# A two-layer decoder trunk: reciprocals by transposed rows, and the first two weight units multiplied together

## The chip, the cores and the metric

The kernel runs on one core of one Trainium2 chip. The core has a matrix engine (TensorE, PE in the profile, with its weight loads as PEld), a vector engine (VectorE, DVE), an activation engine (ScalarE, ACT), GpSimd (POOL) and a queue engine (SyncE, SP) that only starts transfers here. Each engine works through its own instructions in order; semaphores make it wait for others. The metric is the device time of one execution in microseconds (us), as the median of several runs; less is better.

## The reference

512 positions of width 1024 pass two layers. The change lies in the first (even) layer, whose mixer is:

```python
h = x @ w_in                                  # one projection
q_a, c_kv, q_idx, k_idx, w_idx, q_b, k_b, v_b, f_in = split(h)
q_lat = einsum('bshd,hrd->bshr', q_a, w_uk) * HEAD_DIM**-0.5
cum_f = cumsum(log_sigmoid(f_in + b_f))       # forget gates of heads B
# per block of 128 queries:
score = einsum('bth,bths->bts', w_idx, relu(q_idx . k_idx))   # 8 index heads
sel   = top_k(score, 128)                     # causal
oa = softmax(q_lat . c_sel + t5_bias) @ c_sel # 8 heads A, selected keys only
ob = softmax(q_b . k_b + cum_f - cum_f_keys) @ v_b            # 8 heads B
out = concat([oa @ w_uv, ob]) @ w_o
x = layer_norm(ALPHA * x + out); x = layer_norm(ALPHA * x + conv_ffn(x))
```

The second layer has a gated mixer and another such FFN. All data are float32.

## The kernel before

Every float32 operand of a product is split in two rounded parts, high and low, and a product is three matmuls (`mm3`: high x high, high x low, low x high). The splitting is one cast on ACT for the high part and one subtraction for the low part, on DVE, or on POOL for the units listed in `POOL_CUT`.

All weights are one stream `ws` of units of 128 x 1024. `Stream` loads a unit on SP's queue into one of three `raw` buffers (L60), and cuts it (L76, L80, L78 on POOL) into one of three pairs `whi`/`wlo`, or into a `quad`. Unit 0 holds index keys, forget gates and index weights of the query, units 1 to 4 the index queries, unit 5 the latent keys `c_kv`, units 6 to 9 the values of heads B, then pairs of queries and keys, and from unit 23 on the output projection.

At the start `load_x` (L131) loads x, transposed, in eight chunks of 128 x 512 behind the first unit, and cuts each. `proj` then multiplies unit 0 with all eight chunks, and the index queries follow, unit by unit (L373). Four transposes of the gates (L383) stand behind the index queries and ahead of the latent keys; they give `nfq` and `wi`, which the gate bias and the scores use. The scores (`scores`, L426) follow, then the choice of the 128 best keys in rounds on DVE (`choose`), which is threaded through the later work.

Attention runs over 16 heads (0 to 7 are heads B, 8 to 15 heads A) in the loop at L657. For each head the string `SEQ` gives the order in which the pieces are written: `L` logits of head h, `B` bias of head h+1 (POOL), `T` the ten transposes of the weights of head h-1 into the three-bank tile `tri` and their cut into `pt`, `S` the softmax of head h (`soft`: minimum on DVE, exponentials with their sums `den` on ACT; `soft2`: the reciprocals), `V` the values of head h-2, and digits for pieces of projections that fill PE in between. The values come out with features on partitions, while a reciprocal belongs to a position, so `rd` (128 x 4) must be turned into rows:

```python
nc.sync.dma_start(rd_d[h].rearrange("a b -> b a"), rd)                # soft2, L593
nc.sync.dma_start(rb[r], rd_d[h].rearrange("a b -> (a b)").partition_broadcast(64))   # values, L626
eng.tensor_tensor(out=t, in0=t, in1=rb, op=ALU.mult)                  # values, odd h, L634
nc.scalar.copy(o[0], t)                                               # L635
```

The write goes to DRAM with its last two dimensions exchanged; the read spreads a head's 512 numbers over 64 partitions. For an odd head the pair of heads is multiplied on POOL (the last on DVE) and cut into an `oq` quad, which the output projection (`out_ln`) takes. L631 copies a head's values out of PSUM.

The tile framework sets the semaphores and orders the instructions of each engine by a timeline of its own, so the order on an engine isn't quite that of the code.

Of the kernel before, what the change touches and what calls it, by code (L numbers as in the profile page):

```python
# [94 lines left out]
def _body(ctx, tc, A):  # L95
# [31 lines left out]

    xq = [[quad(), quad()], [quad(), quad()]]
    ws.load_to(1)

    def load_x(c):  # L131
        for j in range(2):
            r = temp()
            k = 2 * c + j
            nc.sync.dma_start(r, A["xT"][:, k])
            hi, lo = xq[0][k // 4][:, k % 4], xq[1][k // 4][:, k % 4]
            nc.scalar.copy(hi, r)  # L137
            nc.vector.tensor_tensor(out=lo, in0=r, in1=_f(hi), op=ALU.subtract)  # L138

    for c in range(4):  # L140
        load_x(c)
# [196 lines left out]
    with ExitStack() as m0:  # L338
# [7 lines left out]
        misc = quad()  # L346
        w = unit()
        p = proj(w, xq)
# [7 lines left out]
        e = temp()  # L356
        g = slice(64, 72)
# [5 lines left out]
        nc.vector.memset(e[g], 1.0)  # L363
        nc.vector.tensor_tensor_scan(out=cw[g], data0=e[g], data1=z[g], initial=0.0, op0=ALU.mult, op1=ALU.add)
        fk_d = dr.tile([NH, S], F32, name="fk_d")
        nc.gpsimd.dma_start(fk_d, cw[g])
        for k in range(5, 9):
            ws.big[base[0] + k] = quad
# [4 lines left out]
        for m in range(4):  # L373
            p = bank()
            half(unit(), xq, p, 128, S)
# [5 lines left out]
        p = bank()  # L381
        for n in range(NCH):
            nc.tensor.transpose(p[:, n * 128:n * 128 + 128], cw[:, n * 128:n * 128 + 128], ident)  # L383
        p3 = p.rearrange("p (a b) -> p a b", a=4)
        nfq = mc.tile([128, NCH, NH], F32)
        nc.scalar.mul(nfq, p3[:, :, 64:72], -1.0)
        wi = mc.tile([128, NCH, NH], F32)
        nc.scalar.mul(wi, p3[:, :, 96:104], float(NH ** -0.5))
# [26 lines left out]
                                compare_op=ALU.is_ge, fill=BIG, base=0, channel_multiplier=1)  # L415

# [158 lines left out]
        rd_d = dr.tile([16, NCH, 128], F32, name="rd_d")  # L575

        def soft(h):

            d, lg = st_[h]
            mn = sm.tile([128, 4], F32, name="mn")  # L580
            den = sm.tile([128, 4], F32, name="den")
            rd = sm.tile([128, 4], F32, name="rd")
            for j in range(NCH):
                dj = dslice(d, j)
                dve[0] = nc.vector.tensor_tensor_reduce(out=dj, in0=lg[j], in1=dj, scale=1.0, scalar=3e38,
                                               op0=ALU.add, op1=ALU.min, accum_out=mn[:, j:j + 1])
                nc.scalar.activation(dj, dj, AF.Exp, bias=mn[:, j:j + 1], scale=-1.0, accum_out=den[:, j:j + 1])
            st_[h] = (d, den, rd)

        def soft2(h):  # L590
            d, den, rd = st_[h]
            nc.vector.reciprocal(rd, den)
            nc.sync.dma_start(rd_d[h].rearrange("a b -> b a"), rd)  # L593
# [3 lines left out]
        def turn(h):  # L597
            d = st_[h][0]
            p = tri.tile([128, 1536], F32, name="tri")
            for i in range(NCH):  # L600
                for j in range(i, NCH):
                    o = PO[i] + (j - i) * 128
                    nc.tensor.transpose(p[:, o:o + 128], d[:, OFF[j] + i * 128:OFF[j] + i * 128 + 128], ident)
# [7 lines left out]
        def values(h):  # L611
# [4 lines left out]
            o = (oq[-1][:, i % 2], oq[-1][:, 2 + i % 2])  # L616
# [6 lines left out]
            if h % 2 == 0:  # L623
                ot[i] = (temp(), temp())
            t, rb = ot[i]
            nc.sync.dma_start(rb[r], rd_d[h].rearrange("a b -> (a b)").partition_broadcast(64))  # L626
# [5 lines left out]
            if h % 2 == 1:  # L632
                eng = nc.gpsimd if h < 15 else nc.vector
                eng.tensor_tensor(out=t, in0=t, in1=rb, op=ALU.mult)  # L634
                nc.scalar.copy(o[0], t)  # L635
                eng.tensor_tensor(out=o[1], in0=t, in1=_f(o[0]), op=ALU.subtract)
# [20 lines left out]
        for h in range(18):  # L657
            for c in SEQ:
# [4 lines left out]
                elif c == "B":  # L663
                    bias(h + 1)
                elif c == "S" and h < 16:
# [4 lines left out]
                elif c == "T" and 1 <= h <= 16:  # L670
                    turn(h - 1)
                elif c == "V" and h >= 2:
                    values(h - 2)
                elif c.isdigit():
                    fill(int(c))
# [190 lines left out]
```

## Time and profile before

| | us |
|---|---|
| runs, median of three | 1243.87 (1243.27 to 1244.43) |
| profiled execution, its own time | 1240.66 |
| its span | 1238.9 |
| PE busy in the span | 1168.8 (94%) |
| DVE, ACT, POOL busy | 685.8, 463.8, 201.9 |
| mean granted PE clock | 0.971 |

The profile's page is of one execution. A row of the timeline has the start and the duration of an instruction or of several alike, the engine, the source line, the operation with the tiles it writes and reads, their shapes, and in brackets how long the engine stood before it and what ended that. A row of the waits has the engine and line that waited, what it waited for, the total, the number of times and the longest. `SPq` rows are transfers started by SP's queue; the time to landing is in the list of issues.

### The profile page before, as it was taken

To read this page: it belongs to the slowest core of one execution; us is meant where nothing else is said; L and a number is where in the kernel's file an instruction comes from. 1 tells how busy PE (TensorE), PEld (TensorE's weight loads), DVE (VectorE), ACT (ScalarE), POOL (GpSimd) and SP (SyncE) were. 2 spreads that over 40 slices of the span, in tenths; PEclk is the share of its full clock that TensorE was granted. 3 is DMA by queue.
4 is the path that set the end of the run, shared out by engine and by line. 5 is a ranking of instruction groups with operands and counts; after the bars stand their busy time and mean duration, and the time that the engine had idled before them with its cause. 6 is when DMAs were issued, how large, how long until landed. Compare 5 with 4: busy or idle time off the path is not lost. (4 is left out here: it accounts for less than half of the span.)

```text
span 1238.9 us, 14423 instructions
## 1 busy us (share of the span) xinstructions
PE 1168.8 (94%) x5512; PEld 972.1 (78%) x5512; DVE 685.8 (55%) x1120; ACT 463.8 (37%) x693; POOL 201.9 (16%) x254
## 2 busy tenths in 40 slices
PE   7999998535999999999999999999999999999997
PEld 7787886434898888888888788888988888888886
DVE  6779854312656656656223885447565665662236
ACT  7525654422234443443222414233344344342121
POOL 3555653310300000000000420013000000000003
PEclk9999998767999999999999999999999999999999
DMA  6612511225213233234334313354123322344321
GB/s 227 216 66 69 94 14 30 60 61 179 93 60 98 90 102 102 88 106 147 121 118 170 111 52 121 126 184 166 60 94 102 102 88 99 102 140 149 102 85 69
DMA packets 49413, 132.03 MB, mean 107 GB/s; under 512 B 13800, under 2 KB 13808, under 8 KB 49344
## 3 DMA queue, kind: packets, MB, share of 16 engines
q1 hardware_dynamic: 44288, 115.39, 29.5%
q0 software_dynamic: 5056, 15.71, 4.1%
q8 instruction: 43, 0.70, 0.3%
q14 instruction: 26, 0.21, 0.1%
HBM read 122.63 MB, written 10.02 MB: 107 GB/s over the span
## 5 line engine op out<-in xcount | busy, mean ns | idle before, releaser
L156 PE MATMUL bank<-quad,whi 128*128 128x512 f32 (+2 forms) x932 | 356.5, 383 | 6.3 <-ACT quad L137 6.3
L157 PE MATMUL bank<-quad,whi 128*128 128x512 f32 (+2 forms) x932 | 355.6, 382 | 0.5 <-DVE quad L138 0.5
L158 PE MATMUL bank<-quad,wlo 128*128 128x512 f32 (+2 forms) x932 | 355.1, 381 | 0.0
L80 DVE TENSOR_TENSOR wlo<-raw,whi 128x1024 fp32r<-128x1024 f32 x150 | 183.6, 1224 | 291.3 <-ACT whi L76 290.6
L76 ACT CAST whi<-raw 128x1024 fp32r<-128x1024 f32 x161 | 169.6, 1053 | 262.0 <-PE bank L158 115.3
L156 PEld LDWEIGHTS bank<-quad,whi 128*128 128x128 f32 x932 | 176.1, 189 | 41.0 <-ACT quad L137 6.3
L157 PEld LDWEIGHTS bank<-quad,whi 128*128 128x128 f32 x932 | 176.5, 189 | 33.6 <-DVE quad L138 1.1
L158 PEld LDWEIGHTS bank<-quad,wlo 128*128 128x128 f32 x932 | 176.4, 189 | 32.9
L156 PE MATMUL bank<-whi,quad 128*128 128x512 f32 x388 | 151.5, 392 | 17.8 <-ACT temp L631 17.8
L157 PE MATMUL bank<-wlo,quad 128*128 128x512 f32 x388 | 151.6, 391 | 0.0
L158 PE MATMUL bank<-whi,quad 128*128 128x512 f32 x388 | 151.3, 390 | 0.0
L213 POOL DMA_DIRECT2D temp<-x x24 | 13.1, 548 | 567.9 <-ACT quadx L324 424.6
L156 PE MATMUL bank<-quad 128*128 128x512 f32 (+5 forms) x280 | 100.4, 362 | 2.3 <-DVE quad L195 1.4
L157 PE MATMUL bank<-quad 128*128 128x512 f32 (+5 forms) x280 | 98.7, 354 | 0.8 <-DVE quad L80 0.8
L156 PEld LDWEIGHTS bank<-whi,quad 128*128 128x128 f32 x388 | 73.2, 189 | 33.2 <-ACT temp L631 18.0
L158 PE MATMUL bank<-quad 128*128 128x512 f32 (+5 forms) x280 | 98.5, 353 | 0.0
L158 PEld LDWEIGHTS bank<-whi,quad 128*128 128x128 f32 x388 | 73.3, 189 | 15.3
L157 PEld LDWEIGHTS bank<-wlo,quad 128*128 128x128 f32 x388 | 73.3, 189 | 15.2
L293 DVE SCALAR_TENSOR_TENSOR temp<-bank,fcw,temp 128x511 f32<-128x511 f32 x88 | 65.4, 743 | 9.1 <-ACT temp L292 9.1
L80 DVE TENSOR_TENSOR quad<-raw,quad 128x1024 fp32r<-128x1024 f32 x24 | 31.2, 1306 | 68.3 <-ACT quad L76 67.9
L295 DVE SCALAR_TENSOR_TENSOR temp<-bank,fcw,temp 128x510 f32<-128x510 f32 x88 | 65.9, 748 | 3.0
L156 PEld LDWEIGHTS bank<-quad 128*128 128x128 f32 (+1 forms) x280 | 52.6, 189 | 14.6 <-issue 3.6
(148 smaller groups left out, 1293.0 us busy)
## 6 DMA issues: line engine op xcount, KB each, us to landing
raw<-in_ws_dram SPq DMA_DIRECT2D x192, 512.0 KB, 3.5
x<-temp SPq DMA_DIRECT2D x24, 256.0 KB, 2.0
temp<-x POOLq DMA_DIRECT2D x24, 256.0 KB, 3.2
temp<-in_xT_dram SPq DMA_DIRECT2D x8, 256.0 KB, 5.5
temp<-fk_d SPq DMA_DIRECT2D x8, 256.0 KB, 4.4
temp<-rd_d SPq DMA_DIRECT2D x16, 128.0 KB, 4.4
temp<-in_x_dram POOLq DMA_DIRECT2D x8, 256.0 KB, 8.3
quad<-in_ln_g_dram POOLq DMA_DIRECT2D x4, 512.0 KB, 6.0
```

Of the source, the lines that this page charges most:

```text
L76: nc.scalar.copy(hi, t)
L80: dve[0] = nc.vector.tensor_tensor(out=lo, in0=t, in1=_f(hi), op=ALU.subtract)
L156: nc.tensor.matmul(out, a[0], b[0], start=first, stop=False)
L157: nc.tensor.matmul(out, a[0], b[1], start=False, stop=False)
L158: return nc.tensor.matmul(out, a[1], b[0], start=False, stop=last)
L213: nc.gpsimd.dma_start(t, src[n * 128:n * 128 + 128, hf * 512:hf * 512 + 512])
L293: nc.vector.scalar_tensor_tensor(out=t[:, 1:], in0=p[:, :S - 1], scalar=cw[:, j, 1:2], in1=t[:, 1:], op0=ALU.mult, op1=ALU.add)
L295: nc.vector.scalar_tensor_tensor(out=t[:, 2:], in0=p[:, :S - 2], scalar=cw[:, j, 0:1], in1=t[:, 2:], op0=ALU.mult, op1=ALU.add)
```

## The change

There are four edits. The reciprocals of two heads are gathered in one tile of 128 x 8, transposed by PE in `turn`, behind the ten transposes of an odd head, into a free part of `tri`, copied by ACT and written by ACT's queue as eight rows of 512 B. Both reads of the pair (still by SP) are issued when its second head's values are done, and the division is a step of its own, `D`, two heads later (`divide`); it is on POOL for pairs 0 to 3 and on DVE for the others. At the start, the first two units are loaded in halves between the x chunks, and the products of both go through the chunks together, after seven products of a zeroed tile whose result isn't used. The transposes of the gates move behind the latent keys. `POOL_CUT` begins at unit 10 instead of 5.

```diff
-SEQ = "L2BT2SV2"
-POOL_CUT = range(5, 23)
+SEQ = "L2BT2SDV2"
+POOL_CUT = range(10, 23)
+WARM = 7
...
+    FIRST = 2
+    misc = quad()
...
-    ws.load_to(1)
...
+    nc.vector.memset(_f(misc[:, 0]), 0.0)
+    w0 = [(rawp.tile([128, 1024], F32, name="raw"), wp.tile([128, 1024], FR, name="whi"),
+           wp.tile([128, 1024], FR, name="wlo")) for _ in range(FIRST)]
+
+    def load_w(u, hf):
+        c = slice(hf * 512, hf * 512 + 512)
+        raw, hi, lo = (t[:, c] for t in w0[u])
+        nc.sync.dma_start(raw, A["ws"][u][:, c])
+        nc.scalar.copy(hi, raw)
+        nc.vector.tensor_tensor(out=lo, in0=raw, in1=_f(hi), op=ALU.subtract)
...
+    load_w(0, 0)
+    load_x(0)
+    load_w(1, 0)
+    for k in (1, 2, 3):
+        load_x(k)
+    load_w(0, 1)
+    load_x(4)
+    load_w(1, 1)
+    for k in (5, 6, 7):
+        load_x(k)
...
-        w = unit()
-        p = proj(w, xq)
+        q = bank()
+        for _ in range(WARM):
+            nc.tensor.matmul(q, misc[:, 0, :128], misc[:, 0], start=True, stop=True)
+        p0 = [bank() for _ in range(FIRST)]
+        for k in range(8):
+            for u in range(FIRST):
+                a = 128 if u else 0
+                w = w0[u][1:]
+                mm3(p0[u][:, a:], wk(w, k * 128, k * 128 + 128), xk(xq, k, a), k == 0, k == 7)
+        p = p0[0]
...
-        rd_d = dr.tile([16, NCH, 128], F32, name="rd_d")
+        rd_d = dr.tile([8, 2 * NCH, 128], F32, name="rd_d")
...
         def soft2(h):
-            d, den, rd = st_[h]
-            nc.vector.reciprocal(rd, den)
-            nc.sync.dma_start(rd_d[h].rearrange("a b -> b a"), rd)
+            d, den = st_[h]
+            if h % 2 == 0:
+                rds[h // 2] = sm.tile([128, 8], F32, name="rd")
+            o = 4 * (h % 2)
+            nc.vector.reciprocal(rds[h // 2][:, o:o + 4], den)
...
+            if h % 2 == 1:
+                nc.tensor.transpose(p[:8, 1280:1408], rds.pop(h // 2), ident)
+                row = temp()[:8, :128]
+                nc.scalar.copy(row, p[:8, 1280:1408])
+                nc.scalar.dma_start(rd_d[h // 2], row)
...
-            nc.sync.dma_start(rb[r], rd_d[h].rearrange("a b -> (a b)").partition_broadcast(64))
...
             if h % 2 == 1:
-                eng = nc.gpsimd if h < 15 else nc.vector
-                eng.tensor_tensor(out=t, in0=t, in1=rb, op=ALU.mult)
-                nc.scalar.copy(o[0], t)
-                eng.tensor_tensor(out=o[1], in0=t, in1=_f(o[0]), op=ALU.subtract)
+                rb = temp()
+                for e in range(2):
+                    nc.sync.dma_start(rb[64 * e:64 * e + 64], rd_d[i, 4 * e:4 * e + 4].rearrange(
+                        "a b -> (a b)").partition_broadcast(64))
+                ot[i].append(rb)
+
+        def divide(i):
+            t, rb = ot.pop(i)
+            q = oq[i // 2]
+            o = (q[:, i % 2], q[:, 2 + i % 2])
+            eng = nc.gpsimd if i < 4 else nc.vector
+            eng.tensor_tensor(out=t, in0=t, in1=rb, op=ALU.mult)
+            nc.scalar.copy(o[0], t)
+            eng.tensor_tensor(out=o[1], in0=t, in1=_f(o[0]), op=ALU.subtract)
...
-        for h in range(18):
+        for h in range(20):
...
+                elif c == "D" and h >= 4 and h % 2 == 0:
+                    divide(h // 2 - 2)
```

The source lines of the changed kernel are other numbers. SP's queue in the attention, before: L593 writes a head's reciprocals, L626 reads them back, L60 loads a weight unit.

```order
L626 DMA temp<-rd_d 64x512
L60 DMA raw<-in_ws_dram 128x1024 x2
L593 DMA rd_d<-rd 128x4x1
L626 DMA temp<-rd_d 64x512
L60 DMA raw<-in_ws_dram 128x1024
L593 DMA rd_d<-rd 128x4x1
```

The same queue now, with L671 for a read and L61 for a weight unit:

```order
L61 DMA raw<-in_ws_dram 128x1024 x2
L671 DMA temp<-rd_d 64x512 x6
L61 DMA raw<-in_ws_dram 128x1024
L671 DMA temp<-rd_d 64x512 x2
L61 DMA raw<-in_ws_dram 128x1024 x3
L671 DMA temp<-rd_d 64x512 x4
```

The writes have left the queue, and reads stand together in pairs.

ACT at the end of the attention, before: L587 are exponentials, L194 cuts the transposed weights, L631 copies values out, L635 cuts a divided pair, L76 casts a weight unit.

```order
L587 ACTIVATE d,den<-d,mn 128x384
L587 ACTIVATE d,den<-d,mn 128x512
L194 CAST pt<-tri 128x1280
L631 COPY temp<-bank 64x512
L635 CAST quad<-temp 128x512
L76 CAST quad<-raw 128x1024 x2
L194 CAST pt<-tri 128x1280
```

ACT at the same place now; L640 copies a pair's row of reciprocals, L641 issues its write, L618 are exponentials, L213 cuts the weights, L667 copies values out, L681 cuts a divided pair, L77 casts a unit.

```order
L640 COPY temp<-tri 8x128
L213 CAST pt<-tri 128x1280
L618 ACTIVATE d,den<-d,mn 128x128
L618 ACTIVATE d,den<-d,mn 128x256
L641 DMA rd_d<-temp 8x128
L618 ACTIVATE d,den<-d,mn 128x384
L667 COPY temp<-bank 64x512
L618 ACTIVATE d,den<-d,mn 128x512
L213 CAST pt<-tri 128x1280
L667 COPY temp<-bank 64x512
L681 CAST quad<-temp 128x512
L77 CAST quad<-raw 128x1024 x2
```

The write of the pair of heads 12 and 13 stands between exponentials of head 15, and the cut L681 behind it is the cut of that same pair.

PE at the start, before, where unit 0 ends and unit 1 begins (L156, L157, L158 are the three products of `mm3`):

```order
L156 MATMUL bank<-quad,whi 128x512
L157 MATMUL bank<-quad,whi 128x512
L158 MATMUL bank<-quad,wlo 128x512
L156 MATMUL bank<-quad,whi 128x384
L157 MATMUL bank<-quad,whi 128x384
```

PE's first rows now (L368 are the products of the zeroed tile, L175, L176, L177 those of `mm3`):

```order
L368 MATMUL bank<-quad 128x512 x7
L175 MATMUL bank<-quad,whi 128x512
L175 MATMUL bank<-quad,whi 128x384
L176 MATMUL bank<-quad,whi 128x512
L177 MATMUL bank<-quad,wlo 128x512
L176 MATMUL bank<-quad,whi 128x384
```

The products of the two units alternate from the first chunk on.

More of the change, by code (lines that the diff above doesn't have):

```diff
@@ L125, in unit, with load_x @@
         return ws.get(i)
+    FIRST = 2
+    misc = quad()
     xq = [[quad(), quad()], [quad(), quad()]]
-    ws.load_to(1)
[L131 to L141, printed above, removed]
+    nc.vector.memset(_f(misc[:, 0]), 0.0)
[7 more added lines that the diff above has]
+        nc.vector.tensor_tensor(out=lo, in0=raw, in1=_f(hi), op=ALU.subtract)
+    def load_x(k):
+        r = temp()
+        nc.sync.dma_start(r, A["xT"][:, k])
+        hi, lo = xq[0][k // 4][:, k % 4], xq[1][k // 4][:, k % 4]
+        nc.scalar.copy(hi, r)
+        nc.vector.tensor_tensor(out=lo, in0=r, in1=_f(hi), op=ALU.subtract)
+    load_w(0, 0)
[8 more added lines that the diff above has]
+        load_x(k)
+    ws.loaded = ws.split_to = base[0] = FIRST
     ident = cst.tile([128, 128], F32)
@@ L356, in _body @@
         e = temp()
+        one = temp()
         g = slice(64, 72)
@@ L362, in _body @@
         nc.vector.scalar_tensor_tensor(out=z[g], in0=z[g], scalar=0.0, in1=e[g], op0=ALU.min, op1=ALU.subtract)
-        nc.vector.memset(e[g], 1.0)
-        nc.vector.tensor_tensor_scan(out=cw[g], data0=e[g], data1=z[g], initial=0.0, op0=ALU.mult, op1=ALU.add)
+        nc.gpsimd.memset(one[g], 1.0)
+        nc.vector.tensor_tensor_scan(out=cw[g], data0=one[g], data1=z[g], initial=0.0, op0=ALU.mult, op1=ALU.add)
         fk_d = dr.tile([NH, S], F32, name="fk_d")
         nc.gpsimd.dma_start(fk_d, cw[g])
-        for k in range(5, 9):
-            ws.big[base[0] + k] = quad
+        for k in range(6, 10):
+            ws.big[k] = quad
         qi = [quad(), quad()]
@@ L373, in _body @@
         for m in range(4):
-            p = bank()
-            half(unit(), xq, p, 128, S)
+            if m < FIRST - 1:
+                p = p0[1 + m]
+            else:
+                p = bank()
+                half(unit(), xq, p, 128, S)
             for s, (a, b) in enumerate(((slice(0, 64), slice(64, 128)), (slice(64, 128), slice(0, 64)))):
@@ L379, in _body @@
                                                in1=_f(qi[s][a, m, lt]), op0=ALU.mult, op1=ALU.subtract)
[L381 to L388, printed above, removed]
         p = proj(unit(), xq)
@@ L415, in _body @@
                                 compare_op=ALU.is_ge, fill=BIG, base=0, channel_multiplier=1)
+        p = bank()
+        for n in range(NCH):
+            nc.tensor.transpose(p[:, n * 128:n * 128 + 128], cw[:, n * 128:n * 128 + 128], ident)
+        p3 = p.rearrange("p (a b) -> p a b", a=4)
+        nfq = mc.tile([128, NCH, NH], F32)
+        nc.scalar.mul(nfq, p3[:, :, 64:72], -1.0)
+        wi = mc.tile([128, NCH, NH], F32)
+        nc.scalar.mul(wi, p3[:, :, 96:104], float(NH ** -0.5))
         sel = [None] + [mc.tile([128, 128 * (j + 1)], F32, name=f"sel{j}") for j in (1, 2, 3)]
@@ L573, in logits @@
             st_[h] = (d, lg)
-        rd_d = dr.tile([16, NCH, 128], F32, name="rd_d")
+        rd_d = dr.tile([8, 2 * NCH, 128], F32, name="rd_d")
+        rds = {}
         def soft(h):
@@ L615, in values @@
             i = h // 2
-            o = (oq[-1][:, i % 2], oq[-1][:, 2 + i % 2])
             v = vB if h < 8 else vA
@@ L623, in values @@
             if h % 2 == 0:
-                ot[i] = (temp(), temp())
-            t, rb = ot[i]
-            nc.sync.dma_start(rb[r], rd_d[h].rearrange("a b -> (a b)").partition_broadcast(64))
+                ot[i] = [temp()]
+            t = ot[i][0]
             for k in range(NCH):
@@ L671, in _body @@
                     turn(h - 1)
-                elif c == "V" and h >= 2:
+                elif c == "V" and 2 <= h <= 17:
                     values(h - 2)
```

4 lines of the change are left out of this document (1 added, 3 removed).

## The prediction

> **What bounds the kernel now.** I read the waits of TensorE (PE) first, then its busy time by stretch, then the queue that the releases lead to. The span:
>
> ```profile
> span 1238.9 us, 14423 instructions
> ```
>
> The profiled execution took 1240.66 us, 1.8 us more than its span and 3.2 us less than the 1243.87 us median of the timed runs. The sum below is made against 1240.66 and then moved by these 3.2 us.
>
> Busy time by stretch (columns: stretch, its length, PE, PEld, DVE, ACT, POOL busy with counts, granted clock, DMA share, GB/s), and below it the longest waits:
>
> ```profile
> 100.00:199.80 99.80, 99.79 (x539) 80.03 (x537) 68.66 (x181) 53.87 (x124) 52.41 (x82) 0.99 0.27 46
> 199.80:292.85 93.05, 42.79 (x210) 34.63 (x210) 28.30 (x62) 33.54 (x70) 23.96 (x35) 0.69 0.27 63
> ...
> POOL temp L634 <- DMA temp<-rd_d: 45.9, 4, 20.0
> ACT quad L635 <- POOL temp L634: 45.2, 5, 13.0
> ...
> PE bank L156 <- ACT pt L194: 26.0, 3, 14.4
> ```
>
> PE never stands between 100 and 199.8 us, then is busy less than half of the next 93 us, at a granted clock of 0.69. The waits chain: PE waits for ACT's cast of the transposed weights (L194), ACT stands in L635 for POOL, POOL stands in L634 for the reciprocals' read from DRAM. ACT and POOL run in order, so what is queued behind L635 and L634 waits too.
>
> Where the read is late shows in SP's queue (start, duration) and the time from issue to landing:
>
> ```profile
> 188.98 0.54 SPq L593 DMA_DIRECT2D rd_d<-rd  x1
> 199.97 0.45 SPq L626 DMA_DIRECT2D temp<-rd_d  x1
> ...
> 284.81 0.45 SPq L626 DMA_DIRECT2D temp<-rd_d  x1
> 285.32 18.75 SPq L60 DMA_DIRECT2D raw<-in_ws_dram  x7
> ...
> x<-temp SPq DMA_DIRECT2D x24, 256.0 KB, 2.0
> temp<-rd_d SPq DMA_DIRECT2D x16, 128.0 KB, 4.4
> rd_d<-rd SPq DMA_DIRECT2D x16, 2.0 KB, 11.0
> fk_d<-temp POOLq DMA_DIRECT2D x1, 16.0 KB, 3.9
> ```
>
> A write of 2 KB of reciprocals (L593) takes 11.0 us, because its transposed pattern is 512 pieces of one number. The read of that head (L626) stands behind it in SP's queue and waits for its landing, and the next head's write stands behind the read. From 199.97 to 284.81 there are eight reads, heads 8 to 15, so a head costs 84.84/7 = 12.1 us in this stretch, whatever the engines could do. The weights of the next stage stand behind the last read, at 285.32:
>
> ```profile
> 291.15 1.04 ACT L76 CAST quad<-raw 128x1024 fp32r<-128x1024 f32 x1 [20.85 <-DMA raw<-in_ws_dram]
> ...
> 292.85 0.80 PE L156 MATMUL bank<-whi,quad 128*128 128x512 f32 x1 [17.80 <-ACT temp L631]
> ```
>
> **The change part by part: the reciprocals.** Removed are 16 writes of 11.0 us and their places in SP's queue. Added are eight PE transposes, eight small ACT copies, eight writes of 8 rows of 512 B issued by ACT, and 8 x 2 reads (16 as before); the division of a pair comes two heads later. How much PE needs in the stretch when nothing holds it, from the starts of values (V), logits (L) and turn (T) of one head and of what follows each:
>
> ```profile
> 184.28 0.40 PE L156 MATMUL bank<-pt,quad 128*128 128x512 f32 x1
> ...
> 186.12 0.45 PE L156 MATMUL bank<-quad,whi 128*128 128x512 f32 x1
> ...
> 229.40 0.33 PE L156 MATMUL bank<-quad 64*128 64x128 f32 x1
> ...
> 231.50 0.45 PE L156 MATMUL bank<-pt,quad 128*64 128x512 f32 x1
> ...
> 252.69 1.32 PE L603 MATMUL tri<-ident,d 128*128 128x128 f32 x10
> 253.76 0.47 PE L157 MATMUL bank<-pt,quad 128*64 128x512 f32 x1
> ```
>
> V 1.84, L 2.10, T 1.07 us. The 210 instructions of the stretch are seven V, six T, four L and six of the twelve products of a fifth (1.2 us), and 11 products of projections at 0.23: 12.9 + 6.4 + 9.6 + 2.5 = 31.4 us. So 93.05 - 31.4 = 61.6 us is waiting and half clock, and no more can be won here.
>
> What is late next is the last but one pair (heads 12 and 13). Its row is written by ACT behind two exponentials of head 15, so its chain starts about where L of head 15 is read. Before that point PE has 31.4 less two T and three V (7.7) = 23.7 us of work. ACT's 33.54 us in the row above hold what had piled up behind L635 and the casts of the tail, so it needs about as much; with 2 us for waits between the two the point lies at 199.8 + 25.7 = 225.5. From there: the write, between 2.0 (x<-temp, a wide write of SP) and 3.9 us (fk_d<-temp, eight rows, but POOL's queue), with the 11.0 of the scattered write as the far end; I take 2.0, since ACT's queue is of SP's kind and the piece is smaller. Two issues of 0.45 and 4.4 to landing make 7.3, with releases 7.8, the division 0.7: ACT's copy can start 8.5 us after that point. What follows it is in the trace already, for the same pair:
>
> ```profile
> 266.06 0.62 ACT L635 CAST quad<-temp 128x512 fp32r<-128x512 f32 x1 [12.96 <-POOL temp L634]
> 266.58 1.99 ACT L76 CAST quad<-raw 128x1024 fp32r<-128x1024 f32 x2
> 268.60 1.23 ACT L194 CAST pt<-tri 128x1280 fp32r<-128x1280 f32 x1
> ...
> 274.63 0.41 PE L158 MATMUL bank<-pt,quad 128*128 128x128 f32 x1
> ```
>
> From ACT's copy at 266.06 to the end of the last V at 275.04 are 9.0 us, with PE waiting and then at half clock; 0.8 for the copy that frees the last bank. So PE enters the output projection at 225.5 + 8.5 + 9.0 + 0.8 = 243.8 instead of 292.85: **-49.0 us**, at most -60.8 (PE never waits, less the new transposes). The weights are loaded by then, since SP no longer holds them. The eight transposes of the reciprocals take a tenth of a T each: **+0.8**. ACT's eight issues are not seen before; at the 0.54 of SP's first row above they are 4 us of a queue that has room outside the tail: 0 in the sum, 4 in the range. The divisions on POOL (pairs 0 to 3) and DVE come two heads, some 16 us, after the row is made, against a chain of 8: nothing.
>
> **The start.** The rows: first product, pitch cold, pitch warm, the second unit, its successor; and the loads.
>
> ```profile
> 6.27 0.80 PE L156 MATMUL bank<-quad,whi 128*128 128x512 f32 x1 [6.27 <-ACT quad L137]
> ...
> 8.64 0.63 PE L156 MATMUL bank<-quad,whi 128*128 128x512 f32 x1
> 9.06 0.63 PE L157 MATMUL bank<-quad,whi 128*128 128x512 f32 x1
> ...
> 13.43 0.40 PE L156 MATMUL bank<-quad,whi 128*128 128x512 f32 x1
> ...
> 15.51 0.33 PE L156 MATMUL bank<-quad,whi 128*128 128x384 f32 x1
> ...
> 19.70 0.33 PE L156 MATMUL bank<-quad,whi 128*128 128x384 f32 x1
> ...
> 5.00:10.00 5.00, 3.18 (x7) 2.20 (x8) 4.00 (x6) 3.93 (x7) 0.34 (x1) 1.00 1.03 352
> ```
>
> Products of 512 columns follow each other at 0.42 us until about 13 and then at 2.08/9 = 0.23 (nine from 13.43 to 15.51); the second unit's 24 take 4.19. Now both units' products share each x chunk. The first needs 0.26 MB less (half a weight unit), 0.75 us at 352 GB/s, and half a cast, 0.5: it starts at 5.0. All 3.15 MB must land: 2.36 MB more than the 0.79 of the old first product (there by 5.6) at 352 GB/s is 12.3; the last chunk's cast, remainder and six products put the end at 14.8. PE alone needs 24 x 0.23 + 4.19 = 9.7 us from 5.0: 14.7. I take 15.7 for some cold products and imperfect overlap: 19.7 - 15.7 = **-4.0 us** (-4.9 to +3.1, see the cold rival). The seven dummies (7 x 0.42 = 2.9 us) stand where PE only waits and cost nothing unless they outlast 5.0; SP's twelve issues run ahead of the landings as its nine did.
>
> On the clock: PE ran cold for some 6.6 us after its first product here. If the dummies begin at 1.5, that puts the warm clock at 8.1, 1.5 us of loss at most, inside my 1.0. [...]
>
> **The scores.** The gates' transposes (four, 0.4 us) and two small copies now stand directly ahead of the scores, up to 0.5 us of delay for DVE's first row there. POOL_CUT moves five remainders from POOL to DVE:
>
> ```profile
> 39.23 5.99 PE L426 MATMUL bank<-quad 128*128 128x256 f32 x34
> 46.71 5.12 PE L426 MATMUL bank<-quad 128*128 128x512 f32 x14 [1.48 <-ACT temp L428]
> ...
> 40.95 2.00 DVE L431 TENSOR_SCALAR sel<-temp,wi 128x256 f32<-128x256 f32 x1 [1.36 <-ACT temp L428]
> ...
> 38.07 4.72 POOL L78 TENSOR_TENSOR wlo<-raw,whi 128x1024 fp32r<-128x1024 f32 x2
> ...
> L80 DVE TENSOR_TENSOR wlo<-raw,whi 128x1024 fp32r<-128x1024 f32 x150 | 183.6, 1224 | 291.3 <-ACT whi L76 290.6
> ```
>
> The 48 score products need 16 x (0.23 + 0.17 + 0.115) = 8.3 us and take 39.23 to 51.83, 12.6. DVE's first small row takes 2.00 us while POOL cuts a unit and ends when POOL does. With five cuts fewer in POOL's backlog (2.36 us each) that overlap mostly goes; DVE's five (1.22 each) fall before 36 us, where it has room. Between 0 and -4.3, less the 0.5: I take **-2.0**, the middle, for DVE's own rows stay. PE is full from there to 199.8, so both gains pass on.
>
> Sum: -49.0 + 0.8 - 4.0 - 2.0 = -54.2; 1240.66 - 54.2 = 1186.5, and 3.2 more for the median: **1189** (1189.7). All after the attention is as before.
>
> **Rivals.** *Late reads* (0.13): the 11.0 us is the price of any write of rd_d, not of its pieces. Then each chain is 9 us longer: 9 on the last pair and, with two heads at some 11 us against a chain of 17, 6 each on pairs 4 and 5: 21 back, 1210. For it: ACT still waits in order at each pair's cut. Against: fk_d, also eight rows, lands in 3.9.
>
> *Cold start* (0.10): gaps between x chunks keep the clock low, so the two units take 24 x 0.42 + 24 x 0.32 (three quarters of the columns) = 17.8 us from 5.0 and end at 22.8: +3.1 instead of -4.0, 1197. For it: in the 93 us stretch a few microseconds of waiting brought half clock back. [...]
>
> *Slower* (0.04): PE now waits in its own order for a reciprocal at eight turns, with the next head's products behind it. It decides from 54.2/8 = 6.8 us per turn on, at 1250 from 7.6.
>
> ```profile
> 227.69 0.18 DVE L592 RECIPROCAL rd<-den 128x4 f32<-128x4 f32 x1 [0.88 <-ACT d L587]
> ...
> 232.76 1.32 PE L603 MATMUL tri<-ident,d 128*128 128x128 f32 x10
> ```
>
> For head 13 the reciprocal is there 6 us before the ten transposes end, so the wait should be nothing.
>
> *No change* (0.03): SP still stands in reads whose rows wait in ACT's queue, and a head costs 12 us again: 1244.
>
> **How the numbers follow.** My case has 0.70, with its own range 1176 to 1202: 60.8 in place of 49.0 and 4.9 in place of 4.0 at the low end, 8 us more for the last pair's chain (3.9 for 2.0, ACT's issues, a POOL-like landing) and no gain at the scores at the high end. The range must take in the cold start and half of the late reads: 1174 to 1209, which leaves out about 0.2. 0.2% (2.5 us) is about what a measurement of this kernel can tell from no change: faster 0.93, same 0.03, slower 0.04.
>
> **What would show it.** After: no PE wait on L194 over 4 us before the last pair; POOL's division without a long wait; rd_d's write landing in 2 to 4 us; SP's raw loads no longer behind reads; one PE gap of 5 to 8 us ahead of the output projection; PE's second unit done near 15.7. I am wrong if a row lands near 11 us, if DVE's or ACT's order makes a new wait per pair, or if the clock stays low until 20 us.

## The result, and the profile after

The changed kernel took 1185.84 us (median; 1182.65 to 1191.79) against 1243.57 us of the kernel before on the same chip: ratio 0.9549, 95% interval [0.9501, 0.9597]. On two more chips the ratio was 0.9613 [0.9590, 0.9636] and 0.9602 [0.9584, 0.9621]. The forecast, 1189.7 against 1243.87, is a ratio of 0.9564 and lies between these. The profiled execution took 1182.65 us, 58.0 us less than that of before; it is the shortest of the fourteen executions of the changed kernel on record, so what follows shows it at its best.

The span, and TensorE's busy time by stretch in the changed kernel (columns as before: length, PE, PEld, DVE, ACT, POOL, granted clock, DMA share, GB/s):

```profile
span 1180.9 us, 14445 instructions
...
100.00:199.80 99.80, 99.80 (x551) 80.20 (x550) 73.40 (x187) 60.38 (x136) 56.62 (x89) 1.00 0.20 63
199.80:236.20 36.40, 31.45 (x196) 25.32 (x194) 25.16 (x56) 26.89 (x59) 11.64 (x21) 1.00 0.30 93
```

What was 93.05 us with 42.79 of work at a clock of 0.69 is now 36.40 us with 31.45 of work at 1.00. The longest waits of PE (total, times, longest):

```profile
PE bank L457 <- ACT far L430: 1.8, 1, 1.8
PE bank L175 <- ACT pt L213: 1.6, 1, 1.6
...
PE bank L175 <- DVE quad L214: 1.4, 1, 1.4
PE bank L175 <- ACT whi L140: 1.3, 1, 1.3
PE bank L175 <- ACT temp L667: 1.2, 1, 1.2
PE tri L636 <- DVE pt L214: 1.2, 2, 1.0
```

No wait is longer than 1.9 us; 14.4 us for one cut (L194) and 17.8 ahead of the output projection are gone. The last but one pair of heads, from the timeline of ACT, SP, DVE and PE:

```profile
219.98 0.25 ACT L640 COPY temp<-tri 8x128 f32<-8x128 f32 x1 [0.96 <-PE tri L638]
...
220.27 0.27 ACTq L641 DMA_DIRECT2D rd_d<-temp  x1
221.26 0.39 ACT L618 ACTIVATE d<-d,mn 128x128 f32<-128x128 f32 x1
...
221.58 1.08 SPq L671 DMA_DIRECT2D temp<-rd_d  x2
...
226.95 0.68 DVE L680 TENSOR_TENSOR temp<-temp 128x512 f32<-128x512 f32 x1
...
236.20 0.50 PE L175 MATMUL bank<-whi,quad 128*128 128x512 f32 x1 [1.16 <-ACT temp L667]
```

and the DMA issues of the reads (KB each, median us to landing):

```profile
temp<-rd_d SPq DMA_DIRECT2D x16, 128.0 KB, 3.1
```

The row's write is issued at 220.27. The first read of it waits for that write and starts at 221.58, so this write landed in at most 1.3 us; over the eight pairs of heads the first read starts 1.3 to 3.6 us behind the write's issue. The division at 226.95 waits for no DMA, and PE enters the output projection at 236.20 instead of 292.85: -56.65 us, of which -2.06 were there when the scores ended.

The start and the scores of the changed kernel, from its timeline:

```profile
1.52 3.35 PE L368 MATMUL bank<-quad 128*128 128x512 f32 x7 [1.52 <-DVE mhalf L169]
5.12 0.79 PE L175 MATMUL bank<-quad,whi 128*128 128x512 f32 x1 [0.24 <-ACT quad L147]
7.20 0.69 PE L175 MATMUL bank<-quad,whi 128*128 128x384 f32 x1 [1.29 <-ACT whi L140]
...
19.55 0.34 PE L175 MATMUL bank<-quad,whi 128*128 128x384 f32 x1
...
42.10 7.66 PE L457 MATMUL bank<-quad 128*128 128x256 f32 x40 [1.82 <-ACT far L430]
42.56 1.12 DVE L462 TENSOR_SCALAR sel<-temp,wi 128x256 f32<-128x256 f32 x1 [0.15 <-ACT temp L459]
49.60 0.39 PE L175 MATMUL bank<-quad 128*128 128x512 f32 x1
```

The stretch from 45 to 50 us (columns as above), first of the kernel before:

```profile
45.00:50.00 5.00, 3.52 (x9) 2.46 (x9) 4.69 (x9) 3.54 (x8) 2.34 (x3) 0.72 0.63 217
```

and of the changed kernel:

```profile
45.00:50.00 5.00, 5.00 (x25) 4.31 (x24) 4.79 (x12) 4.70 (x11) 1.97 (x2) 1.00 0.32 117
```

The first real product starts at 5.12 as forecast, but the next waits 1.29 us for the second unit's first half. The pitch (the time from the start of one product of 512 columns to that of the next) stays at 0.42 until 12.9 as it did before, and the third unit starts at 19.55 instead of 19.70. The scores end 2.06 us earlier; in this execution the clock there was 1.00, in that of before 0.72.

### The profile page after: what moved, and what is told of

It reads as the page before. It is cut to its first block, busy times and chain, and to the rows that moved or that the text cites. A ratio compares the mean times of both kernels' runs of the same rounds, so it can differ in the third digit from the quotient of the medians.

```text
span 1180.9 us, 14445 instructions
## 1 busy us (share of the span) xinstructions
PE 1158.8 (98%) x5527; PEld 965.7 (82%) x5527; DVE 690.8 (59%) x1133; ACT 465.5 (39%) x703; POOL 186.5 (16%) x244
## 5 line engine op out<-in xcount | busy, mean ns | idle before, releaser
L175 PE MATMUL bank<-quad,whi 128*128 128x512 f32 (+2 forms) x932 | 355.2, 383 | 1.5 <-ACT whi L140 1.3
L177 PE MATMUL bank<-quad,wlo 128*128 128x512 f32 (+2 forms) x932 | 354.5, 380 | 0.0
L176 PE MATMUL bank<-quad,whi 128*128 128x512 f32 (+2 forms) x932 | 354.4, 380 | 0.0
L77 ACT CAST whi<-raw 128x1024 fp32r<-128x1024 f32 x159 | 167.5, 1053 | 258.2 <-PE bank L177 110.2
L175 PEld LDWEIGHTS bank<-quad,whi 128*128 128x128 f32 x932 | 175.7, 189 | 37.0 <-ACT whi L140 1.8
L177 PEld LDWEIGHTS bank<-quad,wlo 128*128 128x128 f32 x932 | 176.0, 189 | 32.5 <-issue 0.4
L176 PEld LDWEIGHTS bank<-quad,whi 128*128 128x128 f32 x932 | 176.2, 189 | 32.2
L175 PE MATMUL bank<-whi,quad 128*128 128x512 f32 x388 | 150.7, 390 | 1.2 <-ACT temp L667 1.2
L176 PE MATMUL bank<-wlo,quad 128*128 128x512 f32 x388 | 151.0, 389 | 0.0
L177 PE MATMUL bank<-whi,quad 128*128 128x512 f32 x388 | 150.8, 389 | 0.0
L232 POOL DMA_DIRECT2D temp<-x x24 | 13.1, 548 | 568.1 <-ACT quadx L343 424.6
L175 PE MATMUL bank<-quad 128*128 128x512 f32 (+5 forms) x280 | 99.9, 361 | 1.9 <-DVE quad L214 1.4
L176 PE MATMUL bank<-quad 128*128 128x512 f32 (+5 forms) x280 | 98.3, 352 | 0.6 <-DVE quad L81 0.6
L177 PE MATMUL bank<-quad 128*128 128x512 f32 (+5 forms) x280 | 97.7, 350 | 0.0
L175 PEld LDWEIGHTS bank<-whi,quad 128*128 128x128 f32 x388 | 72.8, 188 | 16.4 <-ACT temp L667 1.3
L177 PEld LDWEIGHTS bank<-whi,quad 128*128 128x128 f32 x388 | 72.8, 188 | 15.2
L176 PEld LDWEIGHTS bank<-wlo,quad 128*128 128x128 f32 x388 | 72.9, 188 | 14.8
L175 PEld LDWEIGHTS bank<-quad 128*128 128x128 f32 (+1 forms) x280 | 52.3, 188 | 14.6 <-issue 3.2
L311 ACT ACTIVATE temp<-bank,fcw 128x512 f32<-128x512 f32 x88 | 60.0, 681 | 10.8 <-PE bank L177 10.8
```

The source lines that it names most:

```text
L77: nc.scalar.copy(hi, t)
L175: nc.tensor.matmul(out, a[0], b[0], start=first, stop=False)
L176: nc.tensor.matmul(out, a[0], b[1], start=False, stop=False)
L177: return nc.tensor.matmul(out, a[1], b[0], start=False, stop=last)
L232: nc.gpsimd.dma_start(t, src[n * 128:n * 128 + 128, hf * 512:hf * 512 + 512])
L311: nc.scalar.mul(t, p, cw[:, j, 2:3])
```

## The experiments

Ratios are to the kernel before, run beside each set; the intervals are 95%. The sets ran on different chips, so they are compared by these ratios; the spread of a set is its longest execution less its shortest.

**Which part of the change.** First the reciprocals alone: the kernel before with the row, the later division (on VectorE from pair 4 on) and the sequence `L2BT2SDV2`, nothing else.

> The kernel before with only the reciprocals changed (one transposed row a pair, written by ScalarE's queue, division two heads later); start, gates' transposes and remainders as before. Theory 1: nearly the whole gain is here. TensorE reaches the output projection some 54.6 us earlier than the 292.85 of before, at about 238, and the time is about 1188, 2 us above the changed kernel. Rival (the prediction's sizes): 48.2 us, at 244.6, time about 1195, with the missing 6 us coming from the start and the scores by some way that the first products do not show.

Measured 1184.87 us, ratio 0.9564 [0.9539, 0.9588], so 54.0 us (51 to 57) of 1239.47. PE enters the output projection here:

```profile
239.40 0.50 PE L156 MATMUL bank<-whi,quad 128*128 128x512 f32 x1 [1.57 <-ACT temp L636]
```

That is 53.45 us earlier than before, 0.83 of them from ahead of the attention. Theory 1 holds: this part alone is as good as the whole change. Its four executions spread over 2.7 us, at a mean granted clock of 0.997 in each.

Then everything but the reciprocals: the new start, `POOL_CUT = range(10, 23)` and the gates' transposes at their new place.

> The kernel before with only the new start (two units together, seven dummies), the gates' transposes behind the latent keys and the remainders from unit 10 on; reciprocals as before. Theory 1: TensorE leaves the scores some 2 us earlier, and since it is full until 199.8 the heads bound by SyncE's queue start 2 us earlier too: about 1241.5, ratio 0.998. Rival 1: the chain of SyncE's queue swallows it, 1243.6. Rival 2 (the prediction's sizes): 6 us, 1237.6.

Measured 1235.93 us, ratio 0.9976 [0.9961, 0.9991]: 1.1 to 4.8 us. That is the size of theory 1, but not its way: the trace leaves the scores at 51.58, only 0.1 us before that of the kernel before, with a stretch of low clock between 40 and 55 in both. SP's reads of heads 8 to 15 start 2.15 us earlier for head 8 and 4.68 earlier for head 15 (197.82 and 280.13). The gain is small and real; what moves these reads stays open.

Then the changed kernel with the old start:

```
-    load_w(0, 0); load_x(0); load_w(1, 0); ...      (WARM dummies, two units together)
+    ws.load_to(1); load_x(c) for c in range(4)      (unit 0 whole, then unit 1)
```

> The changed kernel with the old start: the first unit whole, its product complete before the second unit is loaded, no dummies. Theory 1: the new start gives 0.2 us, because the clock stays low until about 13 us in both; second unit done near 19.7 and the time within 1 us of the changed kernel. Rival (the prediction's size): the new start is worth 4 us somewhere, 4 us above the changed kernel.

Measured 1188.32 us, 0.9597 [0.9573, 0.9621]: no more than the changed kernel on the other two chips. Its third unit starts at 19.39, so against the 19.55 of the changed kernel's first trace the new start with its seven dummies is worth nothing. But its trace shows another thing, at the end of the attention (ACT and PE):

```profile
241.78 1.04 ACT L77 CAST quad<-raw 128x1024 fp32r<-128x1024 f32 x1 [2.99 <-DMA raw<-in_ws_dram]
242.84 0.58 ACT L638 COPY temp<-bank 64x512 f32<-64x512 f32 x1
...
243.48 0.80 PE L157 MATMUL bank<-whi,quad 128*128 128x512 f32 x1 [5.50 <-ACT temp L638]
```

The copy that frees the last bank stands behind a cast that waits for weights; PE first reads such weights at 267.4, since four units of 24 products at 0.23 come first. PE waits 5.50 us and starts the projection at half pace (0.80). In the changed kernel one cast stands ahead of the copy, not two.

**Why the reciprocals gain.** Three ways to a part of it. The write on another queue:

```
-            nc.sync.dma_start(rd_d[h].rearrange("a b -> b a"), rd)
+            nc.scalar.dma_start(rd_d[h].rearrange("a b -> b a"), rd)
```

> The kernel before with one edit: the scattered write of each head's reciprocals is issued by ScalarE's queue instead of SyncE's. The write still has 512 pieces and still lands some 11 us after its issue; only SyncE's order is freed, so that the next head's write does not stand behind a read that waits. Theory 1 (order on SyncE's queue makes the 12.1 us a head): the reads come closer than 12 us, a head costs 6 to 9 us, and about half to two thirds of the gain comes back: 1208 to 1220. Rival (the 11 us of the landing set a head whatever the queue, since ScalarE and GpSimd run in order and wait for each read): a head still costs 12 us, 1243.

Measured 1203.94 us, 0.9718 [0.9692, 0.9745]. The write's issues, and from the timeline SP's last eight reads (the first, and the last four) and PE:

```profile
rd_d<-rd ACTq DMA_DIRECT2D x16, 2.0 KB, 12.6
```

```profile
185.74 0.44 SPq L626 DMA_DIRECT2D temp<-rd_d  x1
...
223.87 20.09 SPq L626 DMA_DIRECT2D temp<-rd_d  x4
...
255.62 0.79 PE L156 MATMUL bank<-whi,quad 128*128 128x512 f32 x1 [1.53 <-ACT temp L631]
```

The write still lands only after 12.6 us, yet the eight reads start from 185.74 to 243.5, 8.25 us a head instead of 12.1, and 37.2 of the 56.65 us are won. So a landing of 11 us made 12 us a head only through the order on SP's queue, and one word of code gives two thirds of the gain. A fast write left on SP's queue, the other way to break that chain, was not tried.

The division two heads later (on VectorE from pair 4 on), with the scattered writes left on SP:

> The kernel before with one part of the change alone: the division of a pair comes two heads later; the scattered writes stay a head each, on SyncE's queue. Theory 1: SyncE's order still makes a head cost 12 us from head 8 on, so the delay wins little: 1232 to 1244. Rival: it was ScalarE and GpSimd standing in order behind each read that held TensorE, and the delay alone brings half of the gain or more, 1215 or less.

Measured 1236.0 us in one execution, beside 1238.26 of before. SP's reads of heads 8 and 15:

```profile
199.09 0.45 SPq L625 DMA_DIRECT2D temp<-rd_d  x1
...
280.23 0.45 SPq L625 DMA_DIRECT2D temp<-rd_d  x1
```

(280.23 - 199.09)/7 = 11.6 us a head, and a time within the range of the kernel before (1235.38 to 1242.25): the delay alone wins little or nothing.

And the changed kernel with the row undone:

```
-                nc.tensor.transpose(p[:8, 1280:1408], rds.pop(h // 2), ident)
-                row = temp()[:8, :128]
-                nc.scalar.copy(row, p[:8, 1280:1408])
-                nc.scalar.dma_start(rd_d[h // 2], row)
+                nc.scalar.dma_start(rd_d[h // 2].rearrange("a b -> b a"), rds.pop(h // 2))
```

> The changed kernel with one part undone: no transposed row; a pair's reciprocals are written straight from the 128 x 8 tile, 1024 pieces of one number, at the same place of ScalarE's queue, and the division still comes two heads later. Theory 1: the write takes 11 to 20 us instead of 2; pairs 0 to 5 are hidden by the two heads' delay up to about 16 us, and the last pair's chain is 9 to 18 us longer: TensorE reaches the output projection at 250 to 262 and the time is 1198 to 1212. Rival: with its own queue and the delay the pieces no longer matter, 1186 to 1190.

Measured 1196.75 us, 0.9664 [0.9637, 0.9691]. The write's issues, and from the timeline the end of the attention on DVE, SP, ACT and PE:

```profile
rd_d<-rd ACTq DMA_DIRECT2D x8, 4.0 KB, 11.4
```

```profile
227.44 0.69 DVE L677 TENSOR_TENSOR temp<-temp 128x512 f32<-128x512 f32 x1 [7.17 <-DMA temp<-rd_d]
...
245.94 1.01 SPq L61 DMA_DIRECT2D raw<-in_ws_dram  x2
...
250.23 1.04 ACT L77 CAST quad<-raw 128x1024 fp32r<-128x1024 f32 x1 [9.00 <-DMA raw<-in_ws_dram]
251.93 0.80 PE L175 MATMUL bank<-whi,quad 128*128 128x512 f32 x1 [6.17 <-ACT temp L664]
```

That is just under the 1198 to 1212 of theory 1. 1024 pieces land in 11.4 us, as 512 did in 11.0, so between these the time did not follow the number of pieces. The division that waits 7.17 us is that of heads 10 and 11, the last but two pair: its read starts at 214.39 and lands only at 227.4, while the next pair's scattered write, issued at 216.48, is under way. The last pair's write is issued at 233.18 and lands 11.4 us later; its reads hold SP until then, the weights behind them come at 245.94, and the cast that waits for them holds the last copy. PE enters the projection 12 to 16 us later than in the three traces of the changed kernel. By the ratios the row is worth 0.005 to 0.0115 of 1238, 6 to 14 us, and its place is the end of the attention.

**Why the start gains nothing, and why executions differ.** The changed kernel again, with and without dummies, and with one edge that puts the casts of the projection's later weights behind the last copy:

```
+        if self.hold is not None and i >= self.hold[0]:
+            self.tc.add_manual_dep(c.ins, self.hold[1].ins.name, AFTER, ...)     (tail_order)
```

> The changed kernel once more, beside its variants, to see its spread between executions. Theory 1: its executions fall into two groups some 5 us apart. The copy that frees the last bank of the attention stands behind a cast that waits for weights from DRAM; when these land late, TensorE waits over 3 us ahead of the output projection and runs its first products there at half pace. Expected 1182 to 1184 or 1188 to 1192 on the chip of the first comparison, about 4 us less on the chip where the kernel before took 1239.5. Rival: one group, spread evenly.

> The changed kernel without any dummy. Theory 1: the seven dummies do nothing, because the gaps behind them start the count again: first product at 5.1, pitch 0.23 from about 12.7, second unit done at 19.5 to 20, as with seven. Rival: the seven dummies already save something, and without them the pitch stays at 0.42 until 14 or later and the second unit ends after 21.

> The changed kernel with thirteen dummy products instead of seven, so that TensorE works from 1.5 to about 7 us without a gap. Theory 1: what kept the pitch at 0.42 us until 12.7 were the gaps of 0.24 and 1.29 us behind the seven dummies; the pitch drops to 0.23 some 4.5 to 6 us after 1.5, so before 8.3, and the second unit ends where the last x chunk lets it, at 15.5 to 17 instead of 19.7. Rival 1: dummies on zeros don't count and the pitch drops at 12.3 to 13.3 as in all runs so far; second unit done at 20.5 or later, since the first product starts 2 us later. Of the 3 us won at the start, 1 to 3 reach the end, so that the time is 1 to 3 us less than the changed kernel's on the same chip.

> The changed kernel with one ordering edge: the casts of the output projection's later weights stand behind the copy that frees the last bank of the attention on ScalarE. Theory 1: that copy starts within 0.6 us of the last value product in every execution, TensorE waits at most 1.3 us ahead of the output projection, its first products there follow at 0.23 us, and the slower group of executions is gone: median 0 to 4 us below the changed kernel's, spread under 3 us. Rival: the spread has another cause and stays at 5 to 9 us.

Measured: 1190.33 us (1186.49 to 1191.39), 0.9613; without dummies 1186.54 in one execution; with thirteen 1186.84 (1182.95 to 1190.78), 0.9590 [0.9563, 0.9616]; with the edge 1184.79 (1181.74 to 1188.48), 0.9573 [0.9551, 0.9595]. The landmarks of the traces, in us:

| | pitch 0.23 from | scores begin | next product behind the scores | output projection begins | span |
|---|---|---|---|---|---|
| before | 12.9 | 39.23 | 51.66 | 292.85 | 1238.9 |
| changed | 12.9 | 39.07 | 49.60 | 236.20 | 1180.9 |
| changed, second time | by 7.4 | 36.77 | 51.12 | 239.97 | 1185.9 |
| changed, third time | 10.5 | 37.77 | 50.24 | 237.37 | 1181.6 |
| no dummies | 12.8 | 38.89 | 51.60 | 240.08 | 1184.8 |
| thirteen dummies | by 6.3 | 37.03 | 47.87 | 238.59 | 1187.9 |

With seven dummies the same program has its pitch drop at 12.9, by 7.4 or at 10.5, and its third unit start at 19.55, 17.24 or 18.24: no edit lies between these. Three variants with the same start (the row undone, the edge, everything but the reciprocals) have the drop at 12.8 to 13.1. With thirteen it drops while they run, the third unit starts at 17.50 (forecast 15.5 to 17), the scores begin 2.0 us earlier than in the first trace of the changed kernel and end 1.7 earlier; the early pitch that theory 1 forecast came (6.3, before 8.3). Without dummies nothing is lost against the unlucky case. But what is won early is lost elsewhere: by the times, whose intervals overlap, thirteen dummies can't be told from seven. The granted clock of the changed kernel, second time, in four stretches:

```profile
40.00:45.00 5.00, 3.97 (x15) 3.97 (x16) 3.34 (x6) 4.45 (x15) 2.85 (x2) 0.50 0.65 227
...
45.00:50.00 5.00, 5.00 (x23) 4.53 (x22) 4.74 (x11) 4.53 (x10) 1.72 (x2) 0.83 0.25 80
95.00:105.00 10.00, 8.79 (x37) 6.79 (x38) 9.03 (x29) 5.05 (x11) 2.51 (x2) 0.83 0.45 159
...
240.00:245.00 5.00, 5.00 (x15) 3.98 (x16) 2.53 (x4) 2.35 (x3) 0.54 (x1) 0.66 0.56 197
```

and with thirteen dummies:

```profile
90.00:105.00 15.00, 13.60 (x51) 10.19 (x50) 10.79 (x35) 6.20 (x15) 4.24 (x2) 0.77 0.37 123
230.00:245.00 15.00, 11.68 (x40) 9.32 (x39) 9.13 (x9) 7.60 (x10) 2.81 (x6) 0.66 0.66 210
```

Around 42, 95 and 231 PE waits 1.4 to 1.9 us in all five traces of the changed kernel and its two variants here, and in some the clock then stands at half. At 40 to 50 the loss is 0.50 x 5 + 0.17 x 5 = 3.35 us, so 6.7 us at half clock; at 95 to 105 and at 240 to 245 it is 1.7, so 3.4 us each. The first trace of the changed kernel has none of these.

The trace's own record of clock changes is sharper than these stretches: in that second trace the granted clock is 0.50 from 39.92 to 46.75, 97.94 to 101.36 and 241.30 to 244.72, and in the trace of the kernel before from 47.15 to 50.57, 98.35 to 101.77 and 204.17 to 210.99 at first. In the latter all 13 changes lie whole multiples of 3.413 us after the first entry at 13.02, those named 10, 11, 25, 26, 56 and 58 times; in the first trace of the changed kernel the one change, at 1176.93, lies 341 times 3.413 us after the first entry at 12.98. What brings half clock on was not shown: behind the wait of 1.40 us around 95 it follows in 10 of the 13 traces that have this wait, but neither in the first nor in the third trace of the changed kernel.

The mean granted clock of single executions goes with the spread. Of the fourteen executions of the changed kernel, the five at 0.992 or more took 1182.65 to 1187.63 us, the nine at 0.991 or less 1187.85 to 1191.95.

The expectation of two groups from the last copy alone was too narrow: the copy is one of several places. With the edge PE waits 0.67 us ahead of the projection and has no half clock there in its trace, and the median is 5.5 us under that of the changed kernel on the same chip (the intervals overlap a little). The spread stays at 6.7 us where under 3 was expected.

The reciprocals alone bear on this too: 0.9564 [0.9539, 0.9588] beside 0.9613 [0.9590, 0.9636] and 0.9602 [0.9584, 0.9621] of the changed kernel. Added to the reciprocals the other edits show no gain in any set, and beside the second set, whose interval just clears it, the reciprocals alone are the faster.

**A version that fills the short waits.** From the variant with the edge and thirteen dummies:

```
+                if j == 1 and h == 3:                      # scores
+                    for _ in range(14): nc.tensor.matmul(p[:, 256:], misc[:, 0, :128], misc[:, 0, :256], ...)
+        q = bank()                                         # ahead of the first logits
+        for _ in range(6): nc.tensor.matmul(q, xq[0][0][:, 0, :128], xq[0][0][:, 0], ...)
+            if h == 15:                                    # values of the last head
+                7 dummies behind the values of head 14; then the products with pt's high part first
```

> The changed kernel with the ordering edge on the output projection's casts, thirteen dummies at the start, and dummies where TensorE waits 1.4 to 1.9 us in every execution: 14 of 256 columns behind the first four heads' scores, 6 of 512 ahead of the first logits, 7 ahead of the last head's values, whose products with the high parts now come first. Theory 1: each of these short waits can bring the granted clock to half for about 3.4 us, by chance; with TensorE busy in them the clock stays at 1.00 in all four places, the waits cost nothing more, and the time is 1176 to 1182 with a spread under 4 us, against 1185 to 1191 of the changed kernel on the same chip. Rival: half clock there has another cause (a limit on TensorE's work, which dummies would use up); dips of about 3.4 us stay or move, and the time is within 2 us of the variant with thirteen dummies, 1184 to 1188.

Measured 1180.91 us (1179.63 to 1183.45), 0.9538 [0.9513, 0.9563]. The scores, with L465 the dummies, and the clock:

```profile
39.87 1.84 PE L465 MATMUL bank<-quad 128*128 128x256 f32 x14
41.92 7.74 PE L462 MATMUL bank<-quad 128*128 128x256 f32 x40 [0.21 <-ACT far L435]
```

```profile
45.00:50.00 5.00, 5.00 (x25) 4.09 (x24) 4.58 (x11) 4.60 (x12) 1.72 (x2) 1.00 0.35 124
95.00:105.00 10.00, 10.00 (x50) 7.83 (x50) 9.21 (x34) 6.42 (x17) 2.40 (x1) 1.00 0.36 125
210.00:220.00 10.00, 10.00 (x50) 8.28 (x50) 4.93 (x19) 5.80 (x16) 3.79 (x8) 0.83 0.09 29
```

The wait for `far` is 0.21 instead of 1.82, the clock is 1.00 in the filled places, and the spread is 3.8 us. The mean granted clock of its five executions is 0.996 to 0.998, that of the changed kernel's fourteen 0.987 to 0.998. The one stretch at half clock that is left in the trace, 3.4 us at 210 to 220 (a loss of 1.7), has PE busy throughout, and no wait of PE shows between 190 and 222: waits are not the only thing that such stretches follow. To place this version, the changed kernel a third time:

> The changed kernel a third time, to place it against the variant with the filled waits, whose ratio to the kernel before was 0.9538 [0.9513, 0.9563]. Theory 1: the changed kernel meets up to four half-clock stretches by chance, so its executions lie between 0.954 and 0.963 of the kernel before, with a spread of 5 to 9 us and an interval above 0.9563. Rival: the second set (0.9613) was the chip's, and the ratio is again 0.955 with a spread under 4 us.

Measured 1190.16 us (1183.29 to 1191.95), 0.9602 [0.9584, 0.9621]. The interval lies above that of the version with filled waits. By the ratios this version is 8 to 9 us faster than the changed kernel in its second and third set (0.0064 and 0.0075 of 1238; from the first, wider set it can't be told apart) and 57 us faster than the kernel before. From the reciprocals alone (0.9564 [0.9539, 0.9588]) it can't be told apart. Which of its four edits carries how much was not tried.

## Why the prediction was right, and where its terms were not

1189 was forecast and 1185.84 measured. The place of the gain and its mechanism were right; that the number came so close is in part luck, since two terms missed by -6.4 and +3.85 us and offset each other, and since the next two sets gave 1190.33 and 1190.16 with 46.7 and 49.7 us less than the kernel before.

**The bound** was right: a head cost 12 us because of SP's order. Moving the write off SP, with its landing as late as ever, took that down to 8.25.

**The reciprocals**: forecast -49.0 + 0.8 = -48.2, PE at the projection at 243.8. Measured -54.6 in the first trace, -52.3 and -54.1 in the second and third, -52.6 for this part alone (53.45 - 0.83). The step that failed is "its row is written by ACT behind two exponentials of head 15, so its chain starts about where L of head 15 is read", the point at 225.5. In ACT's order the write does stand behind them; in the trace it is issued at 220.27, 1.0 us before the first of them begins. So the issue came with its own row and not behind that work. That a write of ACT's queue lands like one of SP's was the author's estimate; the scattered write landed in 12.6 us from the one and in 11.0 from the other. With the row's write landing in at most 1.3 us rather than 2.0 and the reads in 3.1 rather than 4.4 (in the traces with scattered writes they take 4.3 to 5.6), the chain of 8.5 us ended before DVE was free. "One PE gap of 5 to 8 us" became gaps of 1.6, 1.0 and 1.2. The result lies midway between the forecast and the bound of -60.8, PE never waiting: counted from the end of the scores the point came 3.2 us earlier than 225.5 says, the chain took 7.4 us and not 8.5, and from ACT's copy to the last value it was 7.4 us and not 9.0.

**The start**: forecast -4.0, measured -0.15 (in the second and third trace -2.46 and -1.46). The step that failed is "if the dummies begin at 1.5, that puts the warm clock at 8.1". They ended at 4.87, gaps of 0.24 and 1.29 us followed, and the pitch dropped at 12.9. The 1.29 was not in the working: the second unit's first half was issued third, at 1.71, and could be cast only at 6.53, with nine more loads behind it in flight, and its product stands ahead of the rest of the first unit's in PE's order. The cold rival came nearer, though its 22.8 was too late by 3. That gaps keep the clock low, as it says, was not shown: in the second trace of the changed kernel gaps of 0.36 and 1.39 us follow the dummies, and the pitch drops by 7.4.

**The scores**: forecast -2.0, measured about -1.9 in the profiles, right for a wrong reason. DVE's first row did shrink, from 2.00 to 1.12 us, but the moved transposes did not simply cost "up to 0.5 us". They exchanged one wait for another:

```profile
41.58 0.47 ACT L424 ACTIVATE temp<-bank 8x384 f32<-8x384 f32 x1
41.96 0.15 ACT L430 ACTIVATE far<-bank 128x8 f32<-128x8 f32 x1
42.02 0.17 ACT L444 ACTIVATE nfq<-bank 128x32 f32<-128x32 f32 x1
```

In all nine traces with the transposes at the new place and no dummies among the scores PE stops after eight score products until the copy `far` (a short one, ahead of the two small copies on ACT) frees its bank, 1.18 to 1.91 us. With the transposes at the old place it stops there after twelve or not at all (0 to 1.23 us), but later waits 1.5 us more for the scores' own copies. What shortened the stage in that trace is mostly the clock, 1.00 against 0.72. Between traces of like clock it is 0.1 (everything but the reciprocals against the kernel before) to 1.2 (the changed kernel against the reciprocals alone, 49.60 and 50.83).

So the terms missed by -6.4, +3.85 and +0.1, together -2.45: -56.65 at the projection instead of -54.2. The last 1.4 us of the 58.0 came behind it, where the first products now follow at full pace (0.50 us for the first, 0.80 before). *Late reads* was tried with 1024 pieces: 1196.75 instead of 1210. Of the eight divisions only that of heads 10 and 11 waits for its read, so the two heads' delay hid the landing for the pairs ahead of it. *No change* and *slower* did not come: no turn waits for a reciprocal. The upper end of the prediction's own case, 1202, is not the sum of its named parts: 8 and 2 us above 1189.7 give 1200.

## What to carry to other kernels

SP's queue, which alternated a slow write with a read that waits for it, had a period close to the landing time (12.1 us a head for 11.0). Moving the write to another queue won two thirds of the gain by itself; the rest lay in the last link of the chain, where no later work hides it. At a seam between stages, see what stands ahead of the copy that frees the last buffer: a cast of far-off weights there cost 5.50 us of waiting, and the projection began at half clock. A kernel whose matrix engine is 98% busy had no half clock in one execution until its last 4.0 us (from 1176.9 on, behind the last product), and in another 13.7 us of it in between (6.83, 3.42 and 3.42), so compare traces at like clock before a gain of 2 us is put down to an edit. And run the parts of a change alone: of four edits here one carries nearly all of the gain.

## What the runs showed of the hardware

- Half clock followed short waits by more than their own length: 1.4 to 1.9 us without a product were followed in some executions by 3.4 or 6.8 us at half clock (0.83 over 10 us; 0.50 and 0.83 over 5 each), in others by none. With these waits filled, five executions had a mean granted clock of 0.996 to 0.998 and a spread of 3.8 us; the changed kernel's three sets spread over 4.9 to 9.1. The reciprocals alone, unfilled, spread over 2.7.
- In the trace of the kernel before the granted clock changed 13 times, each a whole multiple of 3.413 us after the first entry at 13.02; its first three half-clock stretches took 3.42, 3.42 and 6.82 us.
- From 5 to 10 us the views give a granted clock of 1.00 for the kernel before and the changed one, although products of 512 columns follow there at 0.42 us. The first entry in the traces' records of clock changes, at 13.02 and 12.98 us, fits the drop of the pitch (about 13 and 12.9).
- A write of 1024 single numbers landed in 11.4 us, one of 512 in 11.0 (10.1 to 12.6 between kernels); eight rows of 512 B in at most 1.3 for one pair, and by the start of the read, 1.3 to 3.6 us later, for every pair.
- Reads of 128 KB landed in 3.1 us (2.7 to 4.4) beside such rows, and in 4.3 to 5.6, up to 12.5, in the traces with scattered writes.
- ScalarE issued a DMA in 0.27 us at 220.27, 1.0 us before exponentials that stand ahead of it in its order had begun (221.26).
